# The 16-blocks of a triangular inverse: one to a partition and solved by doubling, under another plan of places

## The chip, the cores and the metric

One core of a Trainium2 chip (trn2) runs the program. The metric is device time in microseconds (us) of one execution, lower is better; a run is one execution, and the median of the runs is what is compared. Engines: PE (TensorE, matmul), DVE (VectorE), ACT (ScalarE), POOL (GpSimd), SP (SyncE, which issues the DMAs here).

## The reference, cut to what matters

One layer of a recurrent decoder for 1024 prompt tokens and 8 x 4 sample tokens: one projection `h @ w_in`, three branches, gates and a feed-forward part. Two branches need a triangular inverse for each block of tokens. Branch A (gated delta rule) solves `(I + L) sol = rhs` with strictly lower `L`; branch B (RWKV-7) is a scan that the kernel does in chunks of 64 tokens, each with such an inverse too.

```python
    A = jnp.eye(C, dtype=jnp.float32) + L
    rhs = jnp.concatenate([v * beta[..., None], kb * jnp.exp(gc)[..., None]], axis=-1)
    sol = lax.linalg.triangular_solve(A, rhs, left_side=True, lower=True, unit_diagonal=True)
...
    def step(S, xs):                       # branch B, token by token
        sa = jnp.einsum('bhvk,bhk->bhv', S, -kk_t)
        S = (S * w_t[:, :, None, :] + sa[..., None] * (kk_t * a_t)[:, :, None, :]
             + v_t[..., None] * k_t[:, :, None, :])
        o = jnp.einsum('bhvk,bhk->bhv', S, r_t)
```

## The kernel before, in words

Three stages follow one another. First the norm, branch C and the first half of the projections of A and B. Then the **unit stage**: 18 units (128 tokens of two heads of A and four heads of B; two units hold the sample tokens) pass through a loop of 19 rounds. Last come the merge, the output projection and the feed-forward part, where PE multiplies without a break.

In the unit stage `PLAN` is a tuple of places. Each place names steps and a number of **fill steps**: three 128x352 matmuls each, taken from projections that nobody waits for in this stage (`fill.go(f)`). "n" is the round's new unit, "o" the one of the round before; "nr", "or" are steps of branch B (`rwkv_seg`), "ng", "og" of branch A (`gdn_seg`), "ot" of the triangular inverse (`tri`). PE runs in exactly the order in which this code emits (`T.on`); the other engines' queues are ordered by a scheduler, by priority and by what it takes to be ready, and each queue then runs strictly in its order.

What one unit does, in the terms used below:

- *prep* (first "nr" and "ng" steps): decays, norms and small products; it ends in the Gram matrices `LA` (branch A, L1302) and `GM` (branch B, L1058, two DVE instructions).
- *load* (`inv16_load`, L840 to L843): sixteen DMAs write the 16x16 diagonal blocks of six 128-row matrices (four of `GM`, two of `LA`) to DRAM, and one DMA spreads them over all partitions as `i16b` (128 x 1536, 768 KB).
- *solve* (`inv16_solve`, L857, L860): 15 columns, one after another, a product and a reduction each, on DVE; the result is `i16u`. The first product is pinned in program order.
- *tri*: six steps on PE with DVE and ACT between them, 16-blocks to 32, 64 and 128; it begins with `ixt` (L866) and the transposed `ix` (L887) and ends in `W` and `TT`.
- *recurrence* (`or`, `og`): with `W` and `TT`, two chunks of branch B and one block of branch A, through states `N` and `St` that pass to the next unit. At its end come two reciprocal roots on POOL by 13 small instructions each (`nwyo` and `nwyr`, L645 to L651), whose results scale `oa` (ACT, L1388) and `k` (DVE, L1199); `zg` (L1393) and `k` (L1209) go out to DRAM.

`wlo` (L343) is the low part of a weight tile, made on POOL in this stage; `wraw` are the weight loads.

Of the kernel before, what the change touches and what calls it, by code (L numbers as in the profile page):

```python
# [428 lines left out]
def build(tc, ap):  # L429
    nc = tc.nc  # L430
    with ExitStack() as ctx:
        k = K(tc, ctx, ap)
        V, A, P, T, S = k.V, k.A, k.P, k.T, k.S
# [180 lines left out]
        t1, t2 = der("t1", 4), der("t2", 4)  # L614
# [67 lines left out]
        t = big()  # L682
# [10 lines left out]
        for b0, nb in ((0, 4), (4, 4), (8, 1)):  # L693
            n = 32 if b0 == 8 else 128
            ps = k.tile(k.pr, [128, 4, 128], "rr", 4)
            for j in range(nb):
# [12 lines left out]
                        in1=gla[:32, 8:9].to_broadcast([32, 8, 4]), op=ALU.mult)  # L709
# [114 lines left out]
        mp = mp_cm.__enter__()  # L824
# [5 lines left out]
        H = [slice(0, 64), slice(64, 128)]  # L830

        def inv16_load(J):

            GM, LA, nb, nt = J["GM"], J["LA"], J["nb"], J["nb"] + 2
            k.n += 1
            dr = tc.dram_tile([128, nt, 16], F32, name=f"scr_i{k.n}")
            for g in range(8):
                x = slice(16 * g, 16 * g + 16)
                q = 16 * (g % 4)
                S.dma_start(dr[x, 0:nb], GM[x, g // 4, 0:nb, q:q + 16])  # L840
                S.dma_start(dr[x, nb:nt], LA[x, :, 0, 16 * g:16 * g + 16])  # L841
            mb = k.tile(mp, [128, 1536], "i16b", 1)[:, :256 * nt]
            S.dma_start(mb, dr.rearrange("(g k) b c -> g (k b c)", k=16).unsqueeze(1).to_broadcast([8, 16, 256 * nt]))  # L843
            J["mb"] = mb.rearrange("p (k b c) -> p k b c", k=16, b=nt)

        def inv16_solve(J):

            mb, nt = J["mb"], J["nb"] + 2  # L850
            e16 = k.c("e16").unsqueeze(1).to_broadcast([128, nt, 16])
            u = k.tile(mp, [128, 6, 16], "i16u", 2)[:, :nt]
            t = k.tile(mp, [128, 6, 16], "i16t", 2)[:, :nt]
            P.tensor_copy(u[:, :, 0:1], e16[:, :, 0:1])
            P.tensor_copy(t, e16)
            for c in range(1, 16):
                m = V.tensor_tensor(out=t[:, :, 0:c], in0=u[:, :, 0:c], in1=mb[:, 0:c, :, c].rearrange("p k b -> p b k"), op=ALU.mult)  # L857
                if c == 1:
                    tc.keep_in_program_order(m)
                V.tensor_reduce(out=u[:, :, c], in_=t[:, :, 0:c + 1], axis=AXX, op=ALU.add)  # L860
            J["u16"] = u

        def expand(out, x, mask, nb, q, e=None):
# [574 lines left out]
        for i in range(19):  # L1440
# [134 lines left out]
        for g in range(NG):  # L1575
# [4 lines left out]
            for j in range(8):  # L1580
# [4 lines left out]
                                                  op=ALU.subtract)  # L1585
# [60 lines left out]
```

## Time and profile before

| | |
|---|---|
| median of 3 runs | 2385.85 us (2377.97 to 2386.32) |
| the profiled execution's own time | 2382.02 us |
| its span, first to last instruction | 2380.2 us |
| PE busy | 2184.3 us (92%) |
| DVE busy | 1178.4 us (50%) |
| ACT, POOL busy | 808.7 us (34%), 508.7 us (21%) |
| mean granted PE clock | 0.936 of full speed |
| DVE L857 (the solve's products) | 270 instructions, 77.2 us; 52.6 us idle ahead of them |

A busy share is a mean over the three stages. PE is busy in nearly all of the last stage, and has its gaps in the unit stage, from about 380 to 1285 us. The granted clock tells which of its two levels (1.2 or 2.4 GHz) PE ran at: 1.00 in a stretch means 2.4 GHz throughout.

### The profile page before, as it was taken

What the parts mean: (1) busy time and instruction counts of PE and PEld (TensorE: products, weight loads), DVE (VectorE), ACT (ScalarE), POOL (GpSimd) and SP (SyncE); (2) the same over time, 40 slices, a digit from 0 to 9 for tenths busy, and PEclk for the clock granted to TensorE, in tenths of its full rate; (3) what the DMA queues carried; (4) which work ended last, traced back from release to release, by engine and by line L of the source; (5) the groups of instructions that cost most, each with busy time, mean ns of one, the idle gap of its engine ahead of it and who ended that gap; (6) DMA issues with size and microseconds to landing.
All of it is one profiled execution on the core that took longest, in us unless ns stands there. A gap on an engine that the chain in (4) does not pass through costs nothing.

```text
span 2380.2 us, 43146 instructions
## 1 busy us (share of the span) xinstructions
PE 2184.3 (92%) x16939; PEld 2039.0 (86%) x16939; DVE 1178.4 (50%) x2724; ACT 808.7 (34%) x1915; POOL 508.7 (21%) x1213
## 2 busy tenths in 40 slices
PE   8999998888678789888888999999999999999997
PEld 7998998676566667677778999999999999999997
DVE  7454345556666554575562037655343433433437
ACT  5464343234343333343332222344122121221234
POOL 3113233334343433333432200022000000000003
PEclk9999999689888887988899999999999999999999
DMA  4213332333222232432323354421111111111114
GB/s 138 72 55 125 102 103 74 104 78 81 65 82 86 78 88 81 97 84 63 88 67 124 116 181 159 155 93 62 45 49 41 49 49 45 45 49 41 49 49 149
DMA packets 149010, 200.14 MB, mean 84 GB/s; under 512 B 36676, under 2 KB 89284, under 8 KB 148808
## 3 DMA queue, kind: packets, MB, share of 16 engines
q1 hardware_dynamic: 148808, 197.40, 27.2%
q8 instruction: 133, 2.18, 0.4%
q14 instruction: 69, 0.57, 0.1%
HBM read 152.61 MB, written 44.72 MB: 83 GB/s over the span
## 4 chain that ended last, share of the span: by engine, by line
PE 48%; DVE 5%; DMA 3%; POOL 2%; issue 2%; SPq 1%; ACT 1%; DVEq 0%; POOLq 0%; ACTq 0%
PE g L259 45%; DMA i16b<-scr_i 2%; PE rr L259 2%; SPq L840 1%; PE sg L259 1%; DVE i16t L857 1%; DVE i16u L860 1%; SPq L841 0%; PE sr L259 0%; DVE hf L1582 0%; DVE ahi L1626 0%; DVE k L1199 0%; DVE k L1038 0%; POOL nwyr L651 0%; DVE wlo L343 0%
## 5 line engine op out<-in xcount | busy, mean ns | idle before, releaser
L259 PE MATMUL g<-hhi,whi 128*128 128x352 f32 x2664 | 904.6, 346 | 13.7 <-DVE z L419 12.6
L259 PE MATMUL g<-hhi,wlo 128*128 128x352 f32 x2568 | 847.7, 330 | 1.7 <-POOL wlo L343 1.7
L259 PE MATMUL g<-hlo,whi 128*128 128x352 f32 x2472 | 817.4, 331 | 4.0 <-DVE hlo L561 2.4
L259 PEld LDWEIGHTS g<-hhi,whi 128*128 128x128 f32 x2664 | 515.8, 195 | 35.3 <-DVE z L419 14.1
L259 PEld LDWEIGHTS g<-hhi,wlo 128*128 128x128 f32 x2568 | 499.7, 195 | 3.1 <-POOL wlo L343 2.3
L259 PEld LDWEIGHTS g<-hlo,whi 128*128 128x128 f32 x2472 | 483.8, 196 | 8.6 <-DVE hlo L561 4.6
L342 ACT CAST whi<-wraw 128x512 fp32r<-128x512 f32 x326 | 200.9, 619 | 538.9 <-PE g L259 526.3
L259 PE MATMUL g<-ahi,wlo 128*128 128x352 f32 x768 | 248.4, 323 | 0.0
L259 PE MATMUL g<-ahi,whi 128*128 128x352 f32 x768 | 248.3, 323 | 0.0
L259 PE MATMUL g<-alo,whi 128*128 128x352 f32 x768 | 248.2, 323 | 0.0
L1547 POOL TENSOR_TENSOR acc<-acc,sq 128x352 f32<-128x352 f32 x36 | 36.9, 1026 | 910.5 <-ACT sq L1546 744.6
L343 DVE TENSOR_TENSOR wlo<-wraw,whi 128x512 fp32r<-128x512 f32 x216 | 151.7, 703 | 160.4 <-ACT whi L342 156.0
L343 POOL TENSOR_TENSOR wlo<-wraw,whi 128x512 fp32r<-128x512 f32 x110 | 145.6, 1326 | 339.5 <-ACT whi L342 335.5
L1608 DVE TENSOR_TENSOR x<-g,x 128x352 f32<-128x352 f32 x192 | 100.4, 524 | 201.2 <-PE g L259 201.2
L259 PEld LDWEIGHTS g<-ahi,wlo 128*128 128x128 f32 x768 | 144.8, 189 | 0.1
L259 PEld LDWEIGHTS g<-ahi,whi 128*128 128x128 f32 x768 | 144.6, 188 | 0.2
L259 PEld LDWEIGHTS g<-alo,whi 128*128 128x128 f32 x768 | 144.6, 188 | 0.1
L1597 DVE TENSOR_TENSOR rl<-rl,g 128x352 f32<-128x352 f32 x96 | 49.8, 519 | 131.0 <-ACT rl L1596 131.0
L857 DVE TENSOR_TENSOR i16t<-i16u,i16b 128x6 f32<-128x6 f32 (+5 forms) x270 | 77.2, 286 | 52.6 <-DMA i16b<-scr_i 45.7
L1596 ACT ACTIVATE rl<-g 128x352 f32<-128x352 f32 x96 | 44.4, 463 | 136.4 <-PE g L259 136.4
L1599 DVE TENSOR_TENSOR alo<-rl,ahi 128x352 fp32r<-128x352 f32 x96 | 50.4, 525 | 47.5 <-ACT ahi L1598 47.5
L1598 ACT CAST ahi<-rl 128x352 fp32r<-128x352 f32 x96 | 46.7, 487 | 63.2 <-DVE rl L1597 63.2
(346 smaller groups left out, 2854.9 us busy)
## 6 DMA issues: line engine op xcount, KB each, us to landing
wraw<-win SPq DMA_DIRECT2D x126, 256.0 KB, 2.8
wraw<-wdn SPq DMA_DIRECT2D x80, 256.0 KB, 2.6
wraw<-wup SPq DMA_DIRECT2D x64, 256.0 KB, 2.7
scr_t<-z SPq DMA_DIRECT2D x24, 528.0 KB, 3.1
tgl<-scr_t SPq DMA_DIRECT2D x24, 528.0 KB, 4.8
i16b<-scr_i SPq DMA_DIRECT2D x16, 768.0 KB
scr_za<-z SPq DMA_DIRECT2D x16, 528.0 KB, 10.4
wraw<-wout SPq DMA_DIRECT2D x32, 256.0 KB, 2.7
```

What stands on the lines that cost most here:

```text
L259: return self._pin(self.eng.matmul(*a, **kw))
L342: self.A.copy(hi, r3)
L343: self.lo_eng.tensor_tensor(out=lo, in0=r3, in1=hi.bitcast(F32), op=ALU.subtract)
L840: S.dma_start(dr[x, 0:nb], GM[x, g // 4, 0:nb, q:q + 16])
L857: m = V.tensor_tensor(out=t[:, :, 0:c], in0=u[:, :, 0:c], in1=mb[:, 0:c, :, c].rearrange("p k b -> p b k"), op=ALU.mult)
L860: V.tensor_reduce(out=u[:, :, c], in_=t[:, :, 0:c + 1], axis=AXX, op=ALU.add)
L1547: (V if last else P).tensor_tensor(out=acc[g], in0=acc[g], in1=sq, op=ALU.add)
L1596: A.activation(out=rl, in_=ps, func=AF.Relu)
L1597: V.tensor_tensor(out=rl, in0=rl, in1=ps, op=ALU.mult)
L1598: A.copy(a[:, gl(g)], rl)
L1599: V.tensor_tensor(out=b[:, gl(g)], in0=rl, in1=a[:, gl(g)].bitcast(F32), op=ALU.subtract)
L1608: V.tensor_tensor(out=x2[c][:, gl(g)], in0=ps, in1=x2[c][:, gl(g)], op=ALU.add)
```

## The change

The load writes 64x64 pieces of `GM` and `LA` to DRAM with four DMAs, at a pitch of 64 x 64 + 64 elements to a matrix, so that one strided DMA fetches every 16-block into a partition of its own: `M` (`i16m`), 48 partitions of 256 elements, in 64-byte pieces. The solve works on 48 partitions: pairs, then 2x2, 4x4 and 8x8 blocks are joined along the free axis by broadcast products and reductions (17 DVE instructions, four of them of 512 elements), from a tile `Z` (`i16z`) that POOL has filled with the identity. `Z` goes back to DRAM in one DMA and comes from there in two as `u` (`i16u`, 64-byte pieces), in the layout that `tri` reads. Load and solve get high priority. The plan has 19 places for 18, the fill steps 38 to a round for 36; the first round has 14 extra ones for 24. The first two steps of `tri` ("nt") stand at the end of the unit's own round, the other four share the first four places of the next, and the recurrence follows at places 3 to 7, ahead of the new unit's `GM`.

```diff
         def inv16_load(J):
...
-            dr = tc.dram_tile([128, nt, 16], F32, name=f"scr_i{k.n}")
-            for g in range(8):
-                x = slice(16 * g, 16 * g + 16)
-                q = 16 * (g % 4)
-                S.dma_start(dr[x, 0:nb], GM[x, g // 4, 0:nb, q:q + 16])
-                S.dma_start(dr[x, nb:nt], LA[x, :, 0, 16 * g:16 * g + 16])
-            mb = k.tile(mp, [128, 1536], "i16b", 1)[:, :256 * nt]
-            S.dma_start(mb, dr.rearrange("(g k) b c -> g (k b c)", k=16).unsqueeze(1).to_broadcast([8, 16, 256 * nt]))
+            w = 64 * 64 + 64
+            dr = tc.dram_tile([2 * nt * w], F32, name=f"scr_i{k.n}")
+            for h in range(2):
+                d = dr[h * nt * w:(h + 1) * nt * w].rearrange("(b x) -> b x", b=nt)[:, 0:64 * 64].rearrange("b (p t) -> p b t", t=64)
+                S.dma_start(d[:, 0:nb], GM[H[h], h, 0:nb, 0:64])
+                S.dma_start(d[:, nb:nt], LA[H[h], :, 0, 64 * h:64 * h + 64])
+            M = J["M"] = k.tile(mp, [48, 272], "i16m", 1)[:8 * nt]
+            src = dr.rearrange("(g x) -> g x", g=8 * nt)[:, 0:16 * 64].rearrange("g (k t) -> g k t", t=64)[:, :, 0:16]
+            S.dma_start(M[:, 0:256], src)
         def inv16_solve(J):
...
-            for c in range(1, 16):
-                m = V.tensor_tensor(out=t[:, :, 0:c], in0=u[:, :, 0:c], in1=mb[:, 0:c, :, c].rearrange("p k b -> p b k"), op=ALU.mult)
-                if c == 1:
-                    tc.keep_in_program_order(m)
-                V.tensor_reduce(out=u[:, :, c], in_=t[:, :, 0:c + 1], axis=AXX, op=ALU.add)
+            Z = k.tile(mp, [48, 272], "i16z", 2)[:r]
+            P.memset(Z, 0.0)
+            P.memset(Z[:, 0:272:17], 1.0)
...
+            def product(out, a, b, n):
+                m = 8 // n
+                p_ = pr_[:, :m * n * n * n].rearrange("p (i r c k) -> p i r c k", i=m, r=n, c=n)
+                for i in range(m):
+                    V.tensor_tensor(out=p_[:, i], in0=a[:, i].unsqueeze(2).to_broadcast([r, n, n, n]),
+                                    in1=b[:, i].rearrange("p k c -> p c k").unsqueeze(1).to_broadcast([r, n, n, n]), op=ALU.mult)
...
+            for n in (4, 8):
+                t = tt[:, :8 * n]
+                product(t, blocks(M, n, 0, n), blocks(Z, n, n, n), n)
+                product(blocks(Z, n, 0, n), blocks(Z, n, 0, 0), t.rearrange("p (i r c) -> p i r c", r=n, c=n), n)
+            k.n += 1
+            dr = tc.dram_tile([2, nt, 64, 16], F32, name=f"scr_i{k.n}")
+            S.dma_start(dr.rearrange("h b (q k) c -> (h b q) (k c)", q=4), Z[:, 0:256])
             u = k.tile(mp, [128, 6, 16], "i16u", 2)[:, :nt]
+            for h in range(2):
+                S.dma_start(u[H[h]], dr[h].rearrange("b p c -> p b c"))
...
-        PLAN = (("nr", 2), ("ng", 2), ("ot", 2), ("ot", 2), ("ot", 2), ("ot ng", 2), ("nr load", 2), ("ot or", 2), ("ot or", 2),
-                ("or og", 2), ("or og", 2), ("or og", 2), ("or unit", 2), ("nr", 2), ("nr solve", 2), ("", 2), ("og", 2), ("or", 2))
+        PLAN = (("nr ot", 2), ("ng ot", 2), ("ot or", 2), ("ot or", 2), ("or og", 2), ("or og", 2), ("or og ng", 2), ("nr load", 2),
+                ("or unit", 2), ("nr", 2), ("nr", 2), ("solve", 2), ("og", 2), ("", 2), ("or", 2), ("", 2), ("", 2), ("nt", 2),
+                ("nt", 2))
...
-                            (inv16_load if w_ == "load" else inv16_solve)(new["J"])
+                            with tc.high_priority():
+                                (inv16_load if w_ == "load" else inv16_solve)(new["J"])
...
-                fill.go(24)
+                fill.go(14)
```

Two places show what moves. The first is DVE's queue at `GM` of a unit late in the stage, before:

```order
L1300 TENSOR_TENSOR ar_12033<-con,gr_11671 128x128
L1300 TENSOR_TENSOR ar_12039<-con,gr_11671 128x128
L1058 TENSOR_TENSOR GM_11428<-rr_11429,con 128x512
L1058 TENSOR_TENSOR GM_11428<-rr_11430,con 128x512
L1144 TENSOR_TENSOR tm_11496<-sr_11495,VT_11112 128x128
L1149 COPY UV_11082<-sr_11495 64x2x64
L1180 TENSOR_TENSOR N_11538<-sr_11495,N_11011 128x128
L1181 TENSOR_TENSOR N_11538<-N_11538,wc_10599 128x128
L1333 SCALAR_TENSOR_TENSOR gtm_11544<-sg_11546,sc,kv_10641 128x128 x2
L1144 TENSOR_TENSOR tm_11562<-sr_11561,VT_11112 128x128
```

The recurrence (`tm`, `UV`, `N`, `gtm`) of the old unit follows `GM` of the new one. The same place with the change:

```order
L1181 TENSOR_TENSOR tm_11289<-sr_11288,VT_10897 128x128
L1186 COPY UV_10867<-sr_11288 64x2x64
L1408 SCALAR_TENSOR_TENSOR St_11320<-St_10725,egl,sg_11273 128x128 x2
L1414 TENSOR_TENSOR oa_11268<-gqs_11272,sg_11273 128x256
L1339 SCALAR_TENSOR_TENSOR LA_11148<-rr_11346,gsl_11181,ar_11348 128x256
L1339 SCALAR_TENSOR_TENSOR LA_11148<-rr_11352,gsl_11181,ar_11354 128x256
L1421 TENSOR_SCALAR oss_11269<-oss_11269 128x2
L1337 TENSOR_TENSOR ar_11956<-con,gr_11445 128x128
L1422 SCALAR_TENSOR_TENSOR oss_11269<-gss_10542,oss_11269 128x2
L1337 TENSOR_TENSOR ar_11962<-con,gr_11445 128x128
L1095 TENSOR_TENSOR GM_11364<-rr_11365,con 128x512
L1095 TENSOR_TENSOR GM_11364<-rr_11366,con 128x512
```

Now the recurrence, up to `St`, `oa` and the sum `oss` that starts `nwyo`, stands ahead of `GM`. The second place is DVE's queue at the end of the solve, with the change:

```order
L880 TENSOR_TENSOR i16p_10909<-i16m_10795,i16z_10906 48x512
L883 TENSOR_REDUCE i16t_10910<-i16p_10909 48x64
L880 TENSOR_TENSOR i16p_10909<-i16z_10906,i16t_10910 48x512
L1246 TENSOR_TENSOR k_1750_10968<-k_1750_10968,zv_9648 128x256
L886 TENSOR_REDUCE i16z_10906<-i16p_10909 48x8x8
L903 TENSOR_TENSOR ixt_11009<-i16u_10930,con 128x192
L924 STREAM_TRANSPOSE ix_11010<-ixt_11009 128x192
L929 TENSOR_TENSOR iy_11011<-rr_11015,con 128x192
```

The last reduction into `Z` and the first reader of `u`, `ixt`, are neighbours in the queue; between them lie `Z`'s way to DRAM and back. What stands in SP's queue for that:

```order
L1433 DMA scr_y<-zg_10248 128x128 x2
L1301 DMA zg_11450<-scr_za_93 128x2x128
L1015 DMA zv_11435<-scr_zb_91 128x2x128
L1249 DMA scr_y<-k_1857_11576 128x128 x2
L894 DMA scr_i_11537<-i16z_11515 48x256
L897 DMA i16u_11539<-scr_i_11537 64x6x16 x2
L337 DMA wraw_12186<-win 128x512
```

Store and loads follow each other, and the next weight load stands behind them.

## Rows read from the trace of the kernel before

**Rows 1.** Head of the page.
```profile
span 2380.2 us, 43146 instructions
```
**Rows 2.** Stretch (us): length, busy of PE, PEld, DVE, ACT, POOL, PEclk, DMA share, GB/s.
```profile
930.00:1285.00 355.00, 302.22 (x3466) 257.71 (x3465) 201.17 (x630) 125.10 (x413) 133.72 (x390) 0.88 0.30 77
1285.00:2380.00 1095.00, 1074.98 (x6673) 1070.40 (x6671) 471.18 (x830) 295.85 (x555) 72.24 (x64) 0.99 0.25 82
```
**Rows 3.** Instructions of line 887: ns min/median/max, first and last start.
```profile
L887 DVE STREAM_TRANSPOSE ix<-ixt x18: 311/378/379, 385.4 to 1250.8; 128x192 f32<-128x192 f32 x16, 128x128 f32<-128x128 f32 x2
```
**Rows 4.** DVE's instructions in time, one late unit: start, duration, instruction, [idle before].
```profile
1020.15 0.38 DVE L887 STREAM_TRANSPOSE ix<-ixt 128x192 f32<-128x192 f32 x1
...
1034.96 1.28 DVE L1058 TENSOR_TENSOR GM<-rr,con 128x512 f32<-128x512 f32 x2
...
1052.90 0.17 DVE L857 TENSOR_TENSOR i16t<-i16u,i16b 128x6 f32<-128x6 f32 x1 [2.27 <-DMA i16b<-scr_i]
...
1057.39 1.46 DVE L1199 TENSOR_TENSOR k<-k,nwyr 128x256 f32<-128x256 f32 x1 [2.12 <-POOL nwyr L651]
...
1062.67 0.41 DVE L1209 TENSOR_TENSOR k<-k,zv 128x256 f32<-128x256 f32 x1
...
1066.11 0.38 DVE L887 STREAM_TRANSPOSE ix<-ixt 128x192 f32<-128x192 f32 x1
```
**Rows 5.** SP's issues of the same unit.
```profile
1042.51 0.63 SPq L843 DMA_DIRECT2D i16b<-scr_i  x1
...
1060.41 1.05 SPq L1396 DMA_DIRECT2D scr_y<-zg  x2
```
**Rows 6.** Chain of waits of the same unit: start, share of the chain.
```profile
1042.51 10.37 DMA i16b<-scr_i
...
1060.78 1.90 DMA scr_y<-zg
```
**Rows 7.** DVE in time: first and last rows of the one solve without other work between.
```profile
377.09 0.17 DVE L857 TENSOR_TENSOR i16t<-i16u,i16b 128x6 f32<-128x6 f32 x1 [6.94 <-DMA i16b<-scr_i]
...
384.96 0.36 DVE L866 TENSOR_TENSOR ixt<-i16u,con 128x192 f32<-128x192 f32 x1
```
**Rows 8.** DMA issues by line: count, KB each, median us to landing.
```profile
gr<-scr_g SPq DMA_DIRECT2D x32, 64.0 KB, 6.4
...
zk<-scr_zb SPq DMA_DIRECT2D x16, 128.0 KB, 2.7
...
scr_i<-GM SPq DMA_DIRECT2D x128, 4.0 KB, 1.4
```
**Rows 9.** POOL in time: first and last of the 26 root instructions.
```profile
1049.25 0.43 POOL L645 TENSOR_SCALAR nwyo<-oss 128x2 int32<-128x2 int32 x1 [14.56 <-DVE mv L1193]
...
1057.15 0.20 POOL L651 TENSOR_TENSOR nwyr<-nwtr,nwyr 128x4 f32<-128x4 f32 x1
```
**Rows 10.** Costliest groups of the page: the weights' low parts, on DVE and POOL.
```profile
L343 DVE TENSOR_TENSOR wlo<-wraw,whi 128x512 fp32r<-128x512 f32 x216 | 151.7, 703 | 160.4 <-ACT whi L342 156.0
L343 POOL TENSOR_TENSOR wlo<-wraw,whi 128x512 fp32r<-128x512 f32 x110 | 145.6, 1326 | 339.5 <-ACT whi L342 335.5
```
**Rows 11.** PE in time, one late unit: recurrence, gap, first and last steps of tri.
```profile
988.30 0.27 PE L259 MATMUL sr<-N,AR 64*64 64x64 f32 x2
...
1003.34 0.68 PE L259 MATMUL rr<-UV,GM 64*64 64x64 f32 x16
...
1013.38 1.12 PE L259 MATMUL rr<-con,k 64*64 64x64 f32 x16 [5.65 <-DVE i16t L857]
...
1020.84 0.45 PE L259 MATMUL rr<-ix,GM 32*32 32x32 f32 x32
...
1030.56 0.48 PE L259 MATMUL rr<-AR,BK 64*128 64x128 f32 x2
```
**Rows 12.** Busy time in the stretch just behind that gap; columns as in group 2.
```profile
1013.40:1018.00 4.60, 4.60 (x35) 3.93 (x36) 4.22 (x16) 1.98 (x6) 0.72 (x1) 0.65 0.10 30
```
**Rows 13.** Chain that ended last: the fill steps left over behind the units, and more.
```profile
1315.20 269.26 PE g L259 x1691
```

More of the change, by code (lines that the diff above doesn't have):

```diff
@@ L844, in inv16_load @@
-            J["mb"] = mb.rearrange("p (k b c) -> p k b c", k=16, b=nt)
-        def inv16_solve(J):
-            mb, nt = J["mb"], J["nb"] + 2
-            e16 = k.c("e16").unsqueeze(1).to_broadcast([128, nt, 16])
-            u = k.tile(mp, [128, 6, 16], "i16u", 2)[:, :nt]
-            t = k.tile(mp, [128, 6, 16], "i16t", 2)[:, :nt]
-            P.tensor_copy(u[:, :, 0:1], e16[:, :, 0:1])
-            P.tensor_copy(t, e16)
-            for c in range(1, 16):
-                m = V.tensor_tensor(out=t[:, :, 0:c], in0=u[:, :, 0:c], in1=mb[:, 0:c, :, c].rearrange("p k b -> p b k"), op=ALU.mult)
-                if c == 1:
-                    tc.keep_in_program_order(m)
-                V.tensor_reduce(out=u[:, :, c], in_=t[:, :, 0:c + 1], axis=AXX, op=ALU.add)
+            w = 64 * 64 + 64
@@ new lines, in inv16_load, with blocks @@
+            S.dma_start(M[:, 0:256], src)
+        def inv16_solve(J):
+            nt = J["nb"] + 2
+            r = 8 * nt
+            M = J["M"]
+            Z = k.tile(mp, [48, 272], "i16z", 2)[:r]
+            P.memset(Z, 0.0)
+            P.memset(Z[:, 0:272:17], 1.0)
+            pr_ = k.tile(mp, [48, 512], "i16p", 1)[:r]
+            tt = k.tile(mp, [48, 64], "i16t", 1)[:r]
+            V.tensor_copy(Z[:, 1:256:34], M[:, 1:256:34])
+            def blocks(a, n, row, col):
+                o = 16 * row + col
+                a = a.rearrange("p (i x) -> p i x", x=34 * n)[:, :, o:o + 16 * n]
+                return a.rearrange("p i (r t) -> p i r t", t=16)[:, :, :, 0:n]
+            R_, a11, a22 = blocks(Z, 2, 0, 2), blocks(Z, 2, 0, 0)[:, :, 0, 1], blocks(Z, 2, 2, 2)[:, :, 0, 1]
+            t2 = tt[:, 0:8].rearrange("p (i c) -> p i c", c=2)
+            V.tensor_copy(R_, blocks(M, 2, 0, 2))
+            V.tensor_tensor(out=t2, in0=R_[:, :, :, 0], in1=a22.unsqueeze(2).to_broadcast([r, 4, 2]), op=ALU.mult)
+            V.tensor_tensor(out=R_[:, :, :, 1], in0=R_[:, :, :, 1], in1=t2, op=ALU.add)
+            V.tensor_tensor(out=t2, in0=R_[:, :, 1], in1=a11.unsqueeze(2).to_broadcast([r, 4, 2]), op=ALU.mult)
+            V.tensor_tensor(out=R_[:, :, 0], in0=R_[:, :, 0], in1=t2, op=ALU.add)
+            def product(out, a, b, n):
[4 more added lines that the diff above has]
+                                    in1=b[:, i].rearrange("p k c -> p c k").unsqueeze(1).to_broadcast([r, n, n, n]), op=ALU.mult)
+                if len(out.shape) == 2:
+                    V.tensor_reduce(out=out, in_=pr_[:, :m * n * n * n].rearrange("p (x k) -> p x k", k=n), axis=AXX, op=ALU.add)
+                    return
+                for i in range(m):
+                    V.tensor_reduce(out=out[:, i], in_=p_[:, i], axis=AXX, op=ALU.add)
+            for n in (4, 8):
[5 more added lines that the diff above has]
+            S.dma_start(dr.rearrange("h b (q k) c -> (h b q) (k c)", q=4), Z[:, 0:256])
+            u = k.tile(mp, [128, 6, 16], "i16u", 2)[:, :nt]
+            for h in range(2):
+                S.dma_start(u[H[h]], dr[h].rearrange("b p c -> p b c"))
```

## The prediction

> **What bounds the kernel now.** The page's head gives the span [rows 1]. Busy time by stretch says where a change can act. In the last stage, 1285 to 2380 us, PE is busy for 1075 of 1095 us at a granted clock of 0.99. Only work taken out of it can shorten it. In the late unit stage, 930 to 1285 us, PE is busy for 302 of 355 us and the clock is 0.88 [rows 2]: here PE waits, so what ends a unit's round sets the time. The starts of `ix`, once per unit, give the round: 18 from 385.4 to 1250.8, 17 periods of 50.9 us on average [rows 3]. One late round, `ix` to `ix` in DVE's queue (1020.15 to 1066.11), lasts 45.96 us [rows 4]. I cut it by DVE's, SP's, the chain's and POOL's rows:
>
> - `ix` end to `GM` end (1036.24): 15.7 us, tri and the new unit's prep.
> - `GM` end to the issue of `i16b` (1042.51): 6.3 us [rows 4, 5]. The sixteen transfers stand ahead of it on SP.
> - Issue to first solve instruction: 10.4 us. The chain of waits has this DMA, 10.37 us [rows 4, 6].
> - First solve instruction to `ix` end: 13.6 us. The 30 instructions take 7.9 us where nothing stands between them [rows 7]; here `k` waits 2.12 us for `nwyr` inside the solve and then takes 1.46 [rows 4].
>
> The load and solve are thus 30.25 of 46 us, and beside them the old unit's recurrence is done for nothing.
>
> **The change, part by part.** It takes load and solve apart and replaces them, but the plan also puts the recurrence behind tri and ahead of the new `GM`. PE and DVE work in order, so the recurrence no longer lies beside the load; it is in series with it. The new round, again `ix` to `ix`:
>
> (a) *`GM` end to solve.* M's transfers are four scatters and a gather instead of sixteen scatters and a 768 KB spread; scatters land in 1.4 us and a plain gather in 2.7 [rows 8], some 5 us with issues. They hide under another wait: in DVE's queue `k` (L1236) and `zg` (L1430) stand ahead of the solve, and they need the roots. The two roots are 26 POOL instructions, 1049.25 to 1057.35 [rows 9], 8.1 us with a break of 0.7, so 7.4 without it. With `oss` ahead of `GM` the first root starts about 1.8 us earlier (`GM`'s own 1.28 and its neighbours): 5.6 us left. POOL also makes `wlo` at 1326 ns [rows 10], and I count two between (2.7), with `zg`'s and `k`'s own 0.4 to 0.5 rounded in: 9.0 us. Ends: 7.0 (one `wlo`, short `k`) and 11.5 (three, `k` at 1.46 again). If the roots came for nothing, M's transfers would be next, at about 5.
>
> (b) *Solve.* 17 instructions for 30. No row shows broadcast products of 48x512. The near rows: 30 instructions in 7.9 us, 0.26 each [rows 7], 13 small ones here at 0.22 = 2.9; and a 512-column DVE operation, 0.703 us [rows 10], or 0.64 for one of `GM`'s two [rows 4]. Four at about 0.69 = 2.8. With the one `k` addition between, 0.41 [rows 4]: 6.1 us. Ends: 4.8 (small ones at the 0.17 of the first row there, large ones at 0.64, no `k`) and 7.9 (no better than now). The rows speak for fewer instructions, but also say that a 512-column one costs three of the small ones. The Trainium skill, "VectorE: DVE Perf Modes", section "The TRN2 errata — SBUF-src ops pay a fixed extra latency per instruction", gives 58 cycles plus one per element at 0.96 GHz for an SBUF operation, and finds by its own measurement 151 plus the elements; by the latter a 512-column one would take 0.69 us, which the 0.703 us agrees with, and the small ones 0.17 or more. By the page (b) would be about 5.4 and the round 0.7 shorter.
>
> (c) *`Z` to DRAM and back as `u`.* New and uncovered: `ixt` stands right behind the last reduction on DVE, and PE has three blank places with six fill steps before tri. Store: `scr_y` of 64 KB was issued at 1060.41 and landed at 1062.68, 2.3 us [rows 5, 6]. Load: 2.7 as `zk` [rows 8]. 5.0 us. Low 3.7 (1.4 + 2.3), high 8.7 (2.3 + the 6.4 of `gr`). I take 5.0: `zk` too is a load of pieces into 128 partitions, while `gr` spreads the same row over all of them, which `u` doesn't.
>
> (d) *`ixt` and `ix`*: 0.36 and 0.38 as now, with the gap 0.8.
>
> (a) to (d) are 20.9 us for 30.25: a gain of 9.4.
>
> (e) *`ix` end to `GM` end.* Two "nt" places and eight of the next round, ten for about six. PE's rows: in the recurrence seven places take 15.04 us (988.30 to 1003.34), 2.15 each; in tri with prep four take 9.72 (1020.84 to 1030.56), 2.43 each [rows 11]. These places hold a step that waits for DVE or ACT, and the plan puts "nr ot", "ng ot" and "or og ng" together, so I take the longer: 24.3. PE idles in (a) to (d): nine places with few steps are about 13 us of work, so 8 of 21 us are a gap. Behind the gap of 5.65 us [rows 11] the granted clock was 0.65 for 4.6 us [rows 12]; between the levels of 1.2 and 2.4 GHz that is 70% at the lower, 3.2 us at half speed, 1.6 lost. It is paid now too, but in a stretch that DVE's solve bounds; afterwards it lies in tri. With `GM`'s 1.28: 27.2 us, for 15.7 now. Ends: 22.8 (2.15, no loss) and 31.9 (2.9 a place).
>
> **Sum.** 20.9 + 27.2 = 48.1 us, 2.1 more than 45.96. The mean of 50.9 says that earlier rounds are longer; they hold other work as well, which the change leaves alone, so I let the difference stand for all 17: +36 us. Fill steps: 38 to a round for 36, 14 extra at the start for 24, so 30 fewer are left behind the units. There 1691 matmuls take 269.26 us [rows 13], 0.159 each; 30 x 3 x 0.159 = 14.3 us less. POOL's two copies become two memsets, SP has 8 transfers for 17 a unit and high priority shifts the queue: all off the path, at nothing: POOL waited 14.56 us ahead of the roots [rows 9], which covers two memsets and is far more than SP needs. Net +22 on the profiled execution's 2382.0: 2404. The median shown is 3.8 higher, so I say **2408 us**.
>
> **Rivals.** 0.5% of 2386 is 12 us, about what a measurement here can tell; with the tail's 14.3 the round must end below 46.1 us for faster and above 47.5 for slower.
>
> *R1, faster: PE runs the ten places without waits.* 45.96 less the gap of 5.65, by 18 places, is 2.24 a place [rows 4, 11]. Two chains, tri and recurrence, then cover each other's latencies, and no clock is lost. (e) = 22.4 + 1.28 = 23.7, the round 44.6: 17 x -1.4 = -23, -14 in the tail, so 2345, shown 2349. For it: the recurrence alone already runs at 2.15. Against it: 2.43 is what tri takes with prep beside it now, and DVE then has the recurrence to do there too. It decides at a round of 46.1, which (a) at its low end gives just as well.
>
> *R2, much slower: 64-byte pieces.* `u` and M move in pieces of 64 bytes. If a load so cut lands like the slowest of its size, `gr` with 6.4 us for 2.7 [rows 8], (c) grows by 3.7, 17 x 3.7 = 63: 2467, shown 2471. Against it: the present scatters write rows of 64 bytes and land in 1.4 us. The Trainium skill, "DMA: Bandwidth & Descriptors", Specifications, says that transfers under 512 B miss line rate and cost a read-modify-write; the 1.4 us of the small scatters does not show that, though those are 4 KB in all.
>
> *R3, no change:* the round grows by 0.8 and the tail's 14.3 gives it back, 2382, shown 2386. It holds for rounds from 46.1 to 47.5: (a) with one `wlo` instead of two.
>
> That the change does not do what it says is small: the solve is shorter by any bound, and the order shows the recurrence ahead of `GM`.
>
> **How the numbers follow.** My forecast 0.40, R1 0.31, R3 0.16, R2 0.13. Slower is forecast and R2, 0.53. The low end reaches some way below R1 (R1 with all low ends of (a) to (c), 4.6 us less a round, would be some 80 us below it and is left out), 2335. The high end takes in 3.1 us more a round (most of (c)'s unknown, or two thirds of (e)'s) but not R2's whole price: 2460. The forecast's own range is 2398 to 2435.
>
> **What would show it.** Right: `ix` starts (L924 there) about 48 us apart late; DVE's `ixt` (L903) idle 4 to 6 us behind DMA `u`; a PE gap of 6 to 8 us ahead of `rr<-ix,GM` and a granted clock near 0.65 behind it; 17 solve instructions in 5 to 6 us; `k` (L1236) still waiting for `nwyr` ahead of the solve; the leftover fill some 90 matmuls shorter. Wrong: a round of 45 us or less with PE's gap under 4 us (R1); `u` landing later than 5 us after its issue (R2); the recurrence beside the solve after all; or rounds unequal, so that early ones gain what late ones lose.

## The result, and the profile after

| | median, us | ratio to before, 95% interval |
|---|---|---|
| before, timed beside it | 2386.09 (4 runs) | 1 |
| changed | 2507.93 (2506.28 to 2511.07, 4 runs) | 1.052 [1.0495, 1.0545] |

The change costs 122 us. The forecast was 2408, the range ended at 2460. The head of the page, and the starts of `ix` (L924 now):

```profile
span 2509.3 us, 42716 instructions
PE 2183.4 (87%) x16939; PEld 2042.7 (81%) x16939; DVE 1178.8 (47%) x2490; ACT 816.8 (33%) x1915; POOL 512.2 (20%) x1213
```
```profile
L924 DVE STREAM_TRANSPOSE ix<-ixt x18: 311/378/379, 380.3 to 1388.8; 128x192 f32<-128x192 f32 x16, 128x128 f32<-128x128 f32 x2
```

PE's busy time is that of before; its gaps grew. Against [rows 1, 3] the span grew by 129.1 us. The first `ix` comes 5.1 us earlier, the 17 rounds take 1008.5 us for 865.4 (143.1 more), and what lies behind the last `ix` takes 1120.5 us for 1129.4 (8.9 less). The whole loss is in the rounds, 59.3 us each for 50.9.

One late round in DVE's queue, from `ix` to `ix` (start, duration, instruction, [idle before]):

```profile
1060.69 0.38 DVE L924 STREAM_TRANSPOSE ix<-ixt 128x192 f32<-128x192 f32 x1
...
1076.27 0.29 DVE L1186 COPY UV<-sr 64x128 f32<-64x128 f32 x1
...
1086.66 0.29 DVE L1186 COPY UV<-sr 64x128 f32<-64x128 f32 x1 [2.92 <-ACT UV L1185]
...
1090.37 1.29 DVE L1095 TENSOR_TENSOR GM<-rr,con 128x512 f32<-128x512 f32 x2 [0.45 <-PE rr L259]
...
1101.01 0.42 DVE L1236 TENSOR_TENSOR k<-k,nwyr 128x256 f32<-128x256 f32 x1 [3.70 <-POOL nwyr L651]
1101.35 0.16 DVE L858 COPY i16z<-i16m 48x8 f32<-48x8 f32 x1
...
1106.89 1.06 DVE L880 TENSOR_TENSOR i16p<-i16z,i16t 48x512 f32<-48x512 f32 x1
1107.88 0.41 DVE L1246 TENSOR_TENSOR k<-k,zv 128x256 f32<-128x256 f32 x1
1108.22 0.67 DVE L886 TENSOR_REDUCE i16z<-i16p 48x64 f32<-48x512 f32 x1
1115.09 0.36 DVE L903 TENSOR_TENSOR ixt<-i16u,con 128x192 f32<-128x192 f32 x1 [6.20 <-DMA i16u<-scr_i]
1115.48 0.38 DVE L924 STREAM_TRANSPOSE ix<-ixt 128x192 f32<-128x192 f32 x1
```

The picture is the one foretold: recurrence (`UV`) ahead of `GM`, then the root, the solve, and the wait for `u`. The sizes are not. From `ix` end to `GM` end 30.6 us (forecast 27.2), to the solve 9.7 (9.0), solve 7.5 (6.1), `u` 6.2 (5.0), `ixt` and `ix` 0.8: 54.8 us for 48.1. PE in the same round:

```profile
1061.12 0.65 PE L259 MATMUL rr<-ix,GM 32*32 32x32 f32 x32 [9.40 <-DVE ix L924]
...
1065.97 0.72 PE L259 MATMUL rr<-ll,lora 64*128 64x128 f32 x8
...
1082.29 1.12 PE L259 MATMUL sr<-N,AR 64*64 64x64 f32 x16 [2.93 <-DVE N L1218]
...
1115.91 0.65 PE L259 MATMUL rr<-ix,GM 32*32 32x32 f32 x32 [10.21 <-DVE ix L924]
```

and its busy time by stretch, columns as in [rows 2]: behind the gap, `ix` to `GM`, the end of that, `GM` to `ix`.

```profile
1060.30:1065.30 5.00, 4.18 (x105) 3.67 (x106) 1.45 (x5) 0.00 (x0) 0.00 (x0) 0.54 0.01 2
1061.07:1091.66 30.59, 26.32 (x344) 22.85 (x344) 18.30 (x44) 12.85 (x44) 10.70 (x27) 0.88 0.20 60
1080.00:1091.66 11.66, 9.37 (x78) 8.49 (x78) 6.75 (x20) 2.76 (x10) 3.15 (x9) 0.85 0.23 62
1091.66:1115.50 23.84, 13.06 (x124) 11.48 (x122) 10.16 (x31) 6.09 (x15) 7.51 (x25) 0.87 0.36 90
```

PE works 13.1 of 23.8 us while solve and `u` are on their way, and then 26.3 of 30.6. Note `rr<-ll,lora` at 1065.97: it is the first PE work of the next unit's prep, and it comes 4.9 us behind the end of `ix`, since two places of tri ("nt") now stand ahead of it. The prediction says nothing of where that step stood before.

### The profile page after: what moved, and what is told of

Same layout as the page of the kernel before. It is cut to its first block, busy times and chain, and to the rows that moved or that the text cites. A ratio compares the mean times of both kernels' runs of the same rounds, so it can differ in the third digit from the quotient of the medians.

```text
span 2509.3 us, 42716 instructions
## 1 busy us (share of the span) xinstructions
PE 2183.4 (87%) x16939; PEld 2042.7 (81%) x16939; DVE 1178.8 (47%) x2490; ACT 816.8 (33%) x1915; POOL 512.2 (20%) x1213
## 5 line engine op out<-in xcount | busy, mean ns | idle before, releaser
L259 PE MATMUL rr<-ix,GM 32*32 32x32 f32 x816 | 19.0, 224 | 171.0 <-DVE ix L924 171.0
L259 PEld LDWEIGHTS rr<-ix,GM 32*32 32x32 f32 x816 | 14.7, 134 | 178.2 <-DVE ix L924 129.3
```

Source lines behind the costliest of these rows:

```text
L259: return self._pin(self.eng.matmul(*a, **kw))
```

## The experiments

For each run the mean of 17 rounds is cut as in the prediction, by DVE's rows (ends of `ix` and `GM`, first and last row of the solve, start of `ixt`). The last column is the median, over the same rounds, of PE's first prep matmul against the end of `ix`. In e4_noroundtrip the solve includes the copy into `u`. The kernel before, timed beside the runs, had 2386.1 us with the result and 2381.4 to 2382.7 with the experiments, so a difference between two rows holds to some 5 us.

| run | median, us | round | ix to GM | GM to solve | solve | to ixt | prep against ix |
|---|---|---|---|---|---|---|---|
| before | 2386 | 50.9 | 15.4 | 22.0 | 12.5 | 0.1 | -4.6 |
| changed | 2508 | 59.3 | 34.7 | 9.3 | 8.7 | 5.8 | +5.3 |
| e1_oldplan | 2351 | 48.8 | 20.4 | 7.1 | 10.4 | 9.7 | +0.4 |
| e2_oldsolve | 2588 | 63.7 | 34.8 | 20.2 | 8.0 | 0.0 | +5.2 |
| e3_fillmoved | 2442 | 55.5 | 31.1 | 10.1 | 7.5 | 5.9 | +4.0 |
| e4_noroundtrip | 2406 | 53.5 | 34.1 | 9.2 | 9.1 | 0.2 | +4.9 |
| e6c_or_nt | 2457 | 55.5 | 24.8 | 8.4 | 11.1 | 10.3 | +5.6 |
| e8_series | 2429 | 54.5 | 27.0 | 9.8 | 8.3 | 8.1 | -14.3 |
| e11_prepfirst | 2485 | 57.6 | 31.9 | 9.3 | 8.7 | 6.2 | -9.9 |
| e13_bothfirst | 2453 | 55.9 | 28.1 | 9.3 | 8.7 | 8.4 | -13.6 |
| e5_fill | 2320 | 47.9 | 19.3 | 7.3 | 11.1 | 8.9 | +0.8 |

**Is it the plan, or the solve with its way through DRAM?** Theory 1 says the plan, theory 2 the way of `Z`. Old plan with the new load and solve:

```diff
...
+        PLAN = (("nr", 2), ("ng", 2), ("ot", 2), ("ot", 2), ("ot", 2), ("ot ng", 2), ("nr load", 2), ("ot or", 2), ("ot or", 2), ("or og", 2), ("or og", 2), ("or og", 2), ("or unit", 2), ("nr", 2), ("nr solve", 2), ("", 2), ("og", 2), ("or", 2))
...
-                fill.go(14)
+                fill.go(24)
```

> The changed kernel with the plan of 18 places and the 24 extra fill steps of before; load, solve and their priority are the new ones. Theory 1 (the plan costs the time, because it puts the recurrence in series with tri and prep; the new load and solve are a gain): DVE's queue has the whole solve among the recurrence, ahead of k and zg, so ix no longer waits for the solve; the round falls from 50.9 us (mean of before) by 5 to 8 us, the time to 2250 to 2300 us. Theory 2 (the way of Z through DRAM and the 64-byte pieces cost it): this kernel has them too, so it is slower than before, 2450 us or more. In both cases the stretch from ix end to GM end goes back to about 15 us.

2350.69 us, ratio to before 0.9876 [0.986, 0.9892]: 1.2% faster than before, by less than the 82 us or more that theory 1 gave it. Theory 2 falls: the same 64-byte pieces, the same way through DRAM, and 31 us gained. In DVE's queue (rows of this run) the solve lies in the recurrence, and `ix` waits for the root alone:

```profile
1008.45 0.17 DVE L858 COPY i16z<-i16m 48x8 f32<-48x8 f32 x1 [2.17 <-DMA i16m<-scr_i]
...
1016.01 0.67 DVE L886 TENSOR_REDUCE i16z<-i16p 48x64 f32<-48x512 f32 x1
...
1024.18 1.53 DVE L1236 TENSOR_TENSOR k<-k,nwyr 128x256 f32<-128x256 f32 x1 [6.05 <-POOL nwyr L651]
1025.63 0.47 DVE L1430 SCALAR_TENSOR_TENSOR zg<-rr,d_hang,zg 128x256 f32<-128x256 f32 x1
1026.02 0.34 DVE L903 TENSOR_TENSOR ixt<-i16u,con 128x192 f32<-128x192 f32 x1
```

From the last row of the solve to `ixt` are 9.3 us, but `ixt` shows no idle time of its own: `u`'s way is hidden behind the wait of `k` for POOL's second root. The round fell by 2.1 us only. One reason is that the roots end late: PE waits 33.6 us for `oa` and 31.2 us for `k` in this run (waits: who for whom, us in total, times, longest), where it waited 10.9 and 8.9 us before. The other is that the stretch from `ix` to `GM` did not go back to 15 us, as expected, but to 20.4: `ix` comes earlier, and prep starts beside it and not 4.6 us ahead.

```profile
PE rr L262 <- ACT oa L1425: 33.6, 21, 4.2
PE rr L259 <- DVE k L1236: 31.2, 16, 3.5
```

The other half, the load and solve of before under the new plan:

```diff
...
+        PLAN = (("nr ot", 2), ("ng ot", 2), ("ot or", 2), ("ot or", 2), ("or og", 2), ("or og", 2), ("or og ng", 2), ("nr load", 2), ("or unit", 2), ("nr", 2), ("nr", 2), ("solve", 2), ("og", 2), ("", 2), ("or", 2), ("", 2), ("", 2), ("nt", 2), ("nt", 2))
...
-                fill.go(24)
+                fill.go(14)
```

> The kernel before (its load and its solve by columns) with the plan of 19 places and 14 extra fill steps. Theory 1: the plan alone makes it slow; from GM end to ix end 16.7 us of load, 7.9 us of solve without gaps and 0.8 us, 25.4 for the 24.6 us (mean) of the changed kernel, so a time of 2510 to 2530 us. Theory 2: without the way through DRAM it loses 5.8 us a round against the changed kernel, 2410 us or less.

2587.54 us, 1.0867 [1.0845, 1.0889]: slower still than theory 1 said (`GM` to solve takes 20.2 us, not 16.7). Its 34.8 us from `ix` to `GM` are those of the changed kernel. So the plan costs 157 us with the new solve (2508 to 2351) and 206 with the old one (2587.5 for 2381.6 beside it), and the new load and solve gain under either plan.

**What the new way costs where it lies on the path.** Store and loads left out, so the inverse isn't computed:

```diff
-            S.dma_start(dr.rearrange("h b (q k) c -> (h b q) (k c)", q=4), Z[:, 0:256])
             u = k.tile(mp, [128, 6, 16], "i16u", 2)[:, :nt]
-            for h in range(2):
-                S.dma_start(u[H[h]], dr[h].rearrange("b p c -> p b c"))
+            P.memset(u, 0.0)
+            V.tensor_copy(u[:r, 0], Z[:, 0:16])
```

> The changed kernel without Z's way to DRAM and back: u is filled with zeros, and a copy of 16 columns of Z into it keeps the order behind the solve (so the inverse is not computed). The store and two loads of each unit are gone. If the way lies on the path with nothing behind it: from the last reduction to ixt 5.8 us become 0.3, 17 x 5.5 = 93 us, 2415 us, still slower than before (theory 1). Theory 2 wants the whole loss of 122 us back, 2390 us or less. If something else is late next (PE's queue), less comes back, 2450 us or more.

2405.84 us, 1.0104 [1.0084, 1.0124]: 102 us back, 5.8 of it in each round, which is the whole of the way's price, and the kernel is still slower than before. Under this plan the way lies on the path with nothing beside it; under the old plan `ixt` doesn't wait for it in the rows above, though no run left it out there.

**What paces `ix` to `GM`.** The fill steps first: ten moved out of that stretch, into the places ahead of "nt".

```diff
...
+        PLAN = (("nr ot", 1), ("ng ot", 1), ("ot or", 1), ("ot or", 1), ("or og", 1), ("or og", 1), ("or og ng", 1), ("nr load", 1), ("or unit", 2), ("nr", 2), ("nr", 2), ("solve", 2), ("og", 4), ("", 4), ("or", 4), ("", 4), ("", 4), ("nt", 1), ("nt", 1))
```

> The changed kernel with the fill steps distributed otherwise: 1 instead of 2 in each of the ten places from the first nt to GM, 4 instead of 2 in the five places ahead of nt; 38 a round as before. If PE's own work paces those ten places (26.4 of 31 us busy in a late round), 10 x 0.48 us leave the path of each round and fall into the gap of 9 to 10 us ahead of ix: 4.8 us a round, 2425 us. If the hand-overs between PE, DVE and ACT pace them, the fill was only in their cover and PE waits instead: 2490 to 2508 us.

2441.62 us, 1.0254 [1.0233, 1.0275]: 66 us back of the 82 that PE's own work alone would give. The stretch fell by 3.6 of 4.8 us, so by the two readings of the expectation PE's own work paces it mostly, and hand-overs the rest.

Then the two moves of the plan, one undone at a time. First the recurrence back behind `GM`, with "nt" still at the end of the round:

```diff
...
+        PLAN = (("nr ot", 2), ("ng ot", 2), ("ot", 2), ("ot ng", 2), ("nr load", 2), ("or", 2), ("or", 2), ("or og", 2), ("or og", 2), ("or og", 2), ("or unit", 2), ("nr", 2), ("nr solve", 2), ("", 2), ("og", 2), ("or", 2), ("nt", 2), ("nt", 2))
...
-                fill.go(14)
+                fill.go(24)
```

> The changed kernel with its two nt places still at the end of the round, but the recurrence back behind GM, beside load and solve (18 places, 36 fill steps a round and 24 extra as before). Theory 1 (the recurrence in series with tri and prep is the loss): ix end to GM end loses four places of work, 34.7 us become 22 to 25, the solve stands ahead of k and zg again, and the time is at the level of the run with the old plan, 2330 to 2370 us. Rival (the nt places are the loss: they put ix and tri at a place where PE can only wait for it): 2450 us or more, with the gap ahead of the first PE step of tri still near 9 us a round.

2457.41 us, 1.031 [1.0288, 1.0333]: neither theory. The stretch fell to 24.8 us as theory 1 said, but the time came back by 51 us only. That is in the rival's range, but its sign is not there: PE waits for `ix` 16.6 us in all, not 9 us a round. PE now waits for something that the old plan hid (waits of this run):

```profile
PE rr L259 <- DVE BK L1082: 74.9, 24, 6.9
PE rr L259 <- DVE k L1236: 40.1, 15, 6.6
```

`BK` is the end of prep's DVE chain. Prep's first PE step stands behind tri's two places (5.5 us behind `ix`), so its chain ends late. In the old plan prep starts earlier (+0.4 in e1_oldplan), its chain runs beside tri, and PE waits 6.7 us in all for `BK`. The same with "nt" ahead of the last recurrence step, so that PE has tri to do while POOL works at the root:

```diff
...
+        PLAN = (("nr ot", 2), ("ng ot", 2), ("ot", 2), ("ot ng", 2), ("nr load", 2), ("or", 2), ("or", 2), ("or og", 2), ("or og", 2), ("or og", 2), ("or unit", 2), ("nr", 2), ("nr solve", 2), ("", 2), ("og", 2), ("nt", 2), ("nt", 2), ("or", 2))
```

> As the one with the recurrence behind GM and nt last, but the two nt places ahead of the round's last recurrence step, which needs the root of k: PE could do tri's first steps while POOL works at the root. If DVE's order allowed it, 2 to 3 us a round less, 2290 to 2320 us. But k and zg stand ahead of ixt in DVE's queue here too, so tri waits for the roots all the same: within 10 us of the other order.

2470.8 us, 1.0362 [1.0333, 1.039]: 13 us slower than with "nt" last. `k` and `zg` stand ahead of `ixt` in DVE's queue in both. The other move undone: "nt" behind prep again, the recurrence still ahead of `GM`.

```diff
...
+        PLAN = (("nr", 2), ("ng", 2), ("ot", 2), ("ot", 2), ("ot", 2), ("ot", 2), ("ot or", 2), ("ot or", 2), ("or og", 2), ("or og", 2), ("or og ng", 2), ("nr load", 2), ("or unit", 2), ("nr", 2), ("nr", 2), ("solve", 2), ("og", 2), ("", 2), ("or", 2))
```

> The changed kernel with one thing undone: tri's first two steps no longer stand at the end of the round ahead of the next unit's prep, but behind prep's first two places, as before; the recurrence still ahead of GM (19 places, 38 fill steps, 14 extra). The run with the recurrence behind GM showed that this alone brings back 51 of 158 us against the old plan. Theory 1a (two losses that add up: prep behind tri's first steps 107 us, the recurrence ahead of GM 51 us): 2400 us, with ix end to GM end, from the first matmul of prep to GM, as long as in the changed kernel (near 26 us late). Theory 1b (either loss alone is the whole one, since the longest chain counts): 2450 to 2510 us. If the recurrence in series costs next to nothing: 2350 us.

2429.0 us, 1.02 [1.0172, 1.0228]: 79 us back, between theories 1a and 1b. One move undone gives 51, the other 79, both (the old plan) 157: two losses that nearly add up, with 27 us that come only when both go. The prediction had seen the recurrence alone. What stays here is PE's wait for `ix`, as long as in the changed kernel (waits of the whole run, changed and e8_series); under the old plan, with the new solve, there is none for this `ix`:

```profile
PE rr L259 <- DVE ix L924: 171.0, 18, 12.6
...
PE rr L259 <- DVE ix L924: 171.9, 17, 13.5
```

A narrower test draws prep's first step of the next unit ahead of "nt", by a new word "xr" in the plan, and leaves everything else:

```diff
...
+        PLAN = (("ot", 2), ("ng ot", 2), ("ot or", 2), ("ot or", 2), ("or og", 2), ("or og", 2), ("or og ng", 2), ("nr load", 2), ("or unit", 2), ("nr", 2), ("nr", 2), ("solve", 2), ("og", 2), ("", 2), ("or", 2), ("", 2), ("", 2), ("xr nt", 2), ("nt", 2))
         new, old = unit(0), None
+        next(new["r"], None)
...
-                        u = new if w_[0] == "n" else old
+                        u = new if w_[0] == "n" else after_ if w_[0] == "x" else old
```

> The changed kernel with one step moved: prep's first step of the next unit (its first PE work, on which its DVE chain rests) is drawn ahead of tri's first two steps instead of behind them. Places, fill steps (38, 14 extra), recurrence ahead of GM, load, solve and Z's way stay. If the changed kernel loses because prep's chain starts only behind tri's first steps (5.3 us behind ix instead of 4.6 us ahead of it), prep's DVE work falls into the wait for u and 5 to 8 us a round come back: 2370 to 2425 us. If what costs is that PE must wait for ix at this place (9 us a round), or the recurrence in series alone, 2480 us or more.

2485.28 us, 1.0435 [1.0401, 1.0469]: 23 us back, a miss. Part of prep's DVE work did go into the wait for `u`. What came up instead is branch A's prep, whose root on POOL now holds DVE's queue ahead of the recurrence's `UV` (DVE's rows of this run):

```profile
1060.40 0.16 DVE L1320 TENSOR_TENSOR gsl<-nwyg 128x2 f32<-128x2 f32 x1 [4.34 <-POOL nwyg L651]
...
1060.99 0.29 DVE L1186 COPY UV<-sr 64x128 f32<-64x128 f32 x1
```

With both prep steps drawn ahead (`xr xg` in the place before "nt"):

```diff
...
+        PLAN = (("ot", 2), ("ot", 2), ("ot or", 2), ("ot or", 2), ("or og", 2), ("or og", 2), ("or og ng", 2), ("nr load", 2), ("or unit", 2), ("nr", 2), ("nr", 2), ("solve", 2), ("og", 2), ("", 2), ("or", 2), ("", 2), ("xr xg", 2), ("nt", 2), ("nt", 2))
         new, old = unit(0), None
+        next(new["r"], None)
+        next(new["g"], None)
```

> The changed kernel with both of prep's first steps of the next unit (branch B's and branch A's, whose end is a root on POOL) drawn ahead of tri's first two steps; the rest as in the changed kernel. If the wait for branch A's root (4.3 us in DVE's queue ahead of UV in the run with branch B's step alone) was what held the stretch from ix to GM, 3 to 4 us a round more come back than there: 2415 to 2435 us, as where tri's two steps were put behind prep. If PE's ten places and the recurrence set it, 2470 to 2490 us as with one step.

2452.52 us, 1.03 [1.0277, 1.0322]: 55 us back in all, 33 of them by branch A's step, which is 1.9 us a round for the 3 to 4 expected. In this order PE's steps follow each other almost as in e8_series, which is 24 us faster; why is open. The stretch fell to 28.1 us; from the solve to `ixt` it rose from 5.8 to 8.4, for prep's rows stand ahead of `ixt` now. With e3's distribution of the fill steps as well:

```diff
...
+        PLAN = (("ot", 1), ("ot", 1), ("ot or", 1), ("ot or", 1), ("or og", 1), ("or og", 1), ("or og ng", 1), ("nr load", 1), ("or unit", 2), ("nr", 2), ("nr", 2), ("solve", 2), ("og", 4), ("", 4), ("or", 4), ("", 4), ("xr xg", 4), ("nt", 1), ("nt", 1))
```

> The same with the fill steps distributed as in the run that moved ten of them out of the ten places from nt to GM (there 66 us less). If with prep out of the stretch PE's own work paces it alone, the whole 10 x 0.48 = 4.8 us a round come back: 80 us less than the run with both steps drawn ahead. If hand-overs between PE, DVE and ACT (tri into recurrence) pace it then, 30 us less or under.

2458.1 us, 1.0321 [1.0296, 1.0346]: nothing. In the late round of its trace the scheduler put prep's rows behind `ix` again when the fill moved, so the run changed two things and tells nothing about either.

**Faster than both.** In the old plan with the new solve the gaps lie ahead of the steps that wait for the roots. Six fill steps moved there:

```diff
...
+        PLAN = (("nr", 2), ("ng", 2), ("ot", 1), ("ot", 1), ("ot", 1), ("ot ng", 1), ("nr load", 2), ("ot or", 1), ("ot or", 1), ("or og", 2), ("or og", 2), ("or og", 2), ("or unit", 2), ("nr", 2), ("nr solve", 2), ("", 5), ("og", 5), ("or", 2))
```

> The run with the old plan, new load and solve, and six of its 36 fill steps moved: one less in each of six places of tri and the first recurrence steps, three more in each of the two places ahead of the steps that wait for the roots (PE's gaps ahead of oa and k sum to 60.7 us there, 3.6 a round). If PE's own work paces tri and prep, 2.9 us a round leave the path: 2300 to 2310 us. If hand-overs pace them: within 10 us of 2350 us.

2319.83 us, 0.973 [0.9708, 0.9751]: 63 us faster than before, timed beside it, and 31 us faster than e1_oldplan, less than the 40 to 50 that PE's own work alone would give. The two waits of e1_oldplan, for `k` and for `oa`, fell to these:

```profile
PE rr L259 <- DVE k L1236: 11.7, 8, 3.3
...
PE rr L262 <- ACT oa L1425: 7.5, 8, 2.5
```

Whether that is the fill or the solve, the kernel before with this plan tells:

```diff
...
+        PLAN = (("nr", 2), ("ng", 2), ("ot", 1), ("ot", 1), ("ot", 1), ("ot ng", 1), ("nr load", 2), ("ot or", 1), ("ot or", 1), ("or og", 2), ("or og", 2), ("or og", 2), ("or unit", 2), ("nr", 2), ("nr solve", 2), ("", 5), ("og", 5), ("or", 2))
```

> The kernel before (its own load and solve, its plan) with the same six fill steps moved as in the fastest version: what the new load and solve are worth by themselves. If the fill's places gave the gain of that version (31 us) whatever the solve, 2350 to 2360 us, and the new load and solve are worth some 31 us in either distribution. If the fill could only fill gaps that the short solve opened: within 12 us of 2385 us, and the two together are worth 65 us.

2352.05 us, 0.9879 [0.9855, 0.9903]. The two add up: the fill's places gain 30 to 31 us with either solve, the new load and solve 31 to 32 us in either distribution. Two attempts to go on from e5_fill did not gain. Prep's first step drawn ahead of the last recurrence step:

```diff
...
+        PLAN = (("", 2), ("ng", 2), ("ot", 1), ("ot", 1), ("ot", 1), ("ot ng", 1), ("nr load", 2), ("ot or", 1), ("ot or", 1), ("or og", 2), ("or og", 2), ("or og", 2), ("or unit", 2), ("nr", 2), ("nr solve", 2), ("", 5), ("og", 5), ("xr", 2), ("or", 0))
         new, old = unit(0), None
+        next(new["r"], None)
...
-                        u = new if w_[0] == "n" else old
+                        u = new if w_[0] == "n" else after_ if w_[0] == "x" else old
```

> The opposite direction from the changed kernel: the fastest version so far (old plan, new load and solve, fill steps moved) with prep's first step of the next unit drawn ahead of the last recurrence step, which waits for POOL's roots. If the place of prep in PE's order sets the round (the changed kernel put it back by tri's two places and lost), prep's chain starts some 3 us a round earlier: 2270 to 2290 us. If k and zg in DVE's queue hold prep up all the same, within 10 us of 2320 us.

2331.67 us, 0.9792 [0.9769, 0.9815]: 12 us slower than e5_fill, a miss. Under this plan, where prep starts beside `ix`, moving it further ahead did not shorten the round. Three more fill steps a round:

```diff
...
+        PLAN = (("nr", 2), ("ng", 2), ("ot", 1), ("ot", 1), ("ot", 1), ("ot ng", 2), ("nr load", 2), ("ot or", 1), ("ot or", 1), ("or og", 2), ("or og", 2), ("or og", 2), ("or unit", 2), ("nr", 2), ("nr solve", 2), ("", 6), ("og", 6), ("or", 2))
```

> The fastest version with three more fill steps a round (39), one of each of two places ahead of the steps that wait for the roots and one ahead of BK's, so 51 steps less behind the units. PE still has 105 us of gaps in its unit stage: if the added steps fall into them, 51 x 0.48 = 24 us less, 2295 us; if they push what follows, 2320 us, since the tail gives back what they take.

2332.5 us, 0.9794 [0.977, 0.9817]: the added steps push what follows (the round is 49.3 us for 47.9), and the tail doesn't give it all back. Behind the last `ix` 84 fill matmuls fewer stand than in e5_fill, 28 steps and not 51, and that stretch is 14 us shorter.

## Why the prediction was wrong, step by step

**What bounds the kernel: right, but read half.** That the round of the unit stage sets the time held in every run. The prediction cut a round by load and solve, and wrote "tri and the new unit's prep" over the rest as one piece. That prep and tri lay side by side in it, with prep first in PE's order, was there to read in the view of [rows 11], between the gap and tri, 4 us ahead of the end of `ix`:

```profile
1016.49 0.77 PE L259 MATMUL rr<-ll,lora 64*128 64x128 f32 x8
```

**(e) is the step that failed.** The text has "ten for about six" places, 2.43 us each, "27.2 us, for 15.7 now". In the round shown, the ten places took (30.59 - 1.29) / 10 = 2.93 us each, the upper end of 2.9: 30.6 us for 27.2, half of the 6.7 us by which this round is longer than the forecast's 48.1. What the sum put at nothing is the place of prep: its start moved from 4.6 us ahead of `ix` to 5.3 behind it (medians). e8_series puts the two tri places behind prep again and gets 79 us back; e13_bothfirst draws prep's two steps alone ahead and gets 55. Over the last seven rounds the stretch has a mean of 30.7 us in the changed kernel, 23.8 in e8_series and 24.1 in e13_bothfirst, both below the 27.2 of the sum. The recurrence, the part that was foreseen, is worth 51 us when it alone is undone.

The base of 15.7 us was a long one of the late rounds (four in a row around it mean 14.2), but that does not enter the time, since the whole round of 45.96 us is at the mean of the last seven, 46.1. To let the difference of the earlier rounds stand for all was right for the round as a whole: it grew by 8.3 us in the first ten and by 8.6 in the last seven. It was not right for the parts. Before, the longer early rounds were longer in load and solve; with the change, in `ix` to `GM` (37.6 us in the first ten). So the means of the table, 15.4 to 34.7, show (e) worse and the rest better than the round shown.

**(a), (b), (c), (d).** Their direction held: the gain of 9.4 us was 10.9 in the mean of the rounds. Their sum did not: in the round shown they took 24.2 us for 20.9, a gain of 6.05 and the other half of the miss. (a) took 9.7 us for 9.0 (9.3 in the mean): `k` waits for `nwyr` ahead of the solve as described. (b) is undersized, 7.5 for 6.1 (8.7 in the mean). Half of that is the product of 512 elements, as DVE's instructions grouped by line and shape show (count, busy us, mean ns, idle before); `zg`, 0.47 us, also lay inside the solve, where the sum had one `k` addition alone:

```profile
L880 DVE TENSOR_TENSOR i16p<-i16z,i16t 48x512 f32<-48x512 f32 x16 | 17.8, 1111 | 0.4
L883 DVE TENSOR_REDUCE i16t<-i16p 48x64 f32<-48x512 f32 x16 | 10.8, 677 | 0.4
```

The reduction is at the 0.69 us taken, the broadcast product at 1.04 (from `i16m`, which has the same count) to 1.11. The rule of the Trainium skill that was weighed there ("VectorE: DVE Perf Modes", "The TRN2 errata — SBUF-src ops pay a fixed extra latency per instruction") gives 0.69 us for an operation on two fp32 operands of 512 elements; the product is not at that, and the reduction, for which that formula isn't given, is. (c) took 6.2 for 5.0 (5.8 in the mean). Store and loads land as the plain rows do or sooner, but SP issued the store 1.2 us behind the last reduction, behind two `scr_y` stores, and the two loads 1.65 us later. A store and a weight load stood between them, which the queue shown with the change does not have:

```profile
1109.12 0.84 SPq L1249 DMA_DIRECT2D scr_y<-k  x2
1110.06 0.37 SPq L894 DMA_DIRECT2D scr_i<-i16z  x1
1110.48 0.42 SPq L1448 DMA_DIRECT2D scr_t<-z  x1
1110.95 0.42 SPq L337 DMA_DIRECT2D wraw<-win  x1
1111.71 1.33 SPq L897 DMA_DIRECT2D i16u<-scr_i  x2
```

e4_noroundtrip confirms the term: 5.8 us a round.

**The clock and the tail.** Behind PE's gap the granted clock was 0.54 for 5 us (forecast 0.65 for 4.6), and behind the shorter gap at 1080 it was 0.85 for 11.7 us more. Over (e) it was 0.88, which is at most 3.7 us lost (an estimate, 0.12 x 30.59; PE also waits in it) for the 1.6 of the sum, so part of (e)'s 3.4 us may be the clock. The tail gave 8.9 us, not 14.3: from the last `ix` on there are 60 fill matmuls fewer (6756 to 6696), not 90.

**The rivals.** R1 (faster) was to show a gap under 4 us; it is 9 to 10. R2's total of 2471 was the nearest, but by luck, for its cause is not there. The DMA issues of the changed kernel (count, KB each, median us to landing):

```profile
i16m<-scr_i SPq DMA_DIRECT2D x16, 48.0 KB, 2.5
scr_i<-i16z SPq DMA_DIRECT2D x16, 48.0 KB, 1.6
i16u<-scr_i SPq DMA_DIRECT2D x32, 24.0 KB, 2.3
```

`i16m` and `i16u`, cut into 64-byte pieces, land as soon as `zk` (2.5 us in the changed kernel); the store of `Z` has rows of 1 KB. The rule cited for R2 (the Trainium skill, "DMA: Bandwidth & Descriptors", Specifications) speaks of the rate, and `u` does move a fifth of `zk`'s bytes in that time; at this size no cost of it shows in the time to landing. R3 and "it does not do what it says" are out.

**The range.** 2460 allowed 3.1 us a round above the forecast, as if one term could miss. In the round shown (e) missed by 3.4, (b) by 1.4, (c) by 1.2 and (a) by 0.7, all upward. Each stayed inside its own ends. Each had been set at the middle of its bounds or below, and the range let one of them miss at a time; it should have added them.

What stays open: the 27 us that come back only when both moves are undone; how much of the loss that is left in e8_series and e13_bothfirst is PE's wait for `ix`, which prep's place did not shorten; and how the stretch from `ix` to `GM` divides between PE's own work and hand-overs once prep is out of it, which e14_bothfill didn't tell.

## What to carry to other kernels

When a step moves in a queue that runs in order, list every chain that starts behind it, not only the one that was moved: here two places of tri slid ahead of another unit's first step, and that chain's late start cost 55 to 79 us, where the recurrence, the move in plain sight, cost 51. Undo the parts of a change one at a time, and the good one shows: the new solve is worth 31 us under the old plan, while the plan that came with it costs 157. If a shorter operation gains little, look at what now ends last (here POOL's roots), and put work that nobody waits for ahead of that wait.

## What the runs showed of the hardware that I had not expected

A DVE product of 48x512 with both operands broadcast took 1.04 to 1.11 us, where a reduction of as many elements took 0.68 and a two-operand operation of 128x512 took 0.70 [rows 10]. Loads of 24 and 48 KB in 64-byte pieces landed in 2.3 and 2.5 us, and `gr`, at 6.4 us before, landed in 3.3 in the changed kernel: its 6.4 was not a property of the transfer.
